# RG-LRU gate products as three passes over split operands, in a two-layer recurrent decoder step

## The chip, the cores and the metric

The kernel runs on one core of a Trainium2 chip. The metric is the device time of one execution in microseconds. Five engines work side by side, each through its own instructions in the order in which the program gives them: PE (TensorE, matmuls), DVE (VectorE), ACT (ScalarE), POOL (GpSimd) and SP (SyncE, which here only issues DMAs). An instruction waits until the semaphores that it names have been raised by other engines or by DMAs, and everything behind it on its engine waits with it.

## What is computed

Two layers run on 320 tokens (a prompt of 256 and eight samples of 8). Each layer normalizes its input, multiplies it with one wide matrix, feeds three branches (S5, RG-LRU, retention) and merges them. The change lies in the RG-LRU branch, whose reference is, shortened:

```python
xc = sum(xp[:, k:k + s] * cw[k] for k in range(CONV_WIDTH)) + conv_b
xb = xc.reshape(bsz, s, LRU_BLOCKS, LRU_BLOCK)            # 8 blocks of 128 channels
r = sigmoid(einsum('bsnc,ncd->bsnd', xb, w_a) + b_a)
i = sigmoid(einsum('bsnc,ncd->bsnd', xb, w_x) + b_x)
log_a = -LRU_C * r * softplus(-lam)
a = exp(log_a)
bx = sqrt(-expm1(2.0 * log_a)) * (i * xc)
h = scan(a, bx)
```

The two einsums are the gate products: per layer and per block of 128 channels one 128x128 matrix for `r` and one for `i`.

## The kernel before, in words

Everything is kept transposed: channels on the 128 partitions, tokens along the row. The program is one stream of weight blocks of 256 output channels (`blocks`, `stream`). A block is cut into chunks of four 128-row slices, a chunk into two half-chunks. A half-chunk is loaded in `raw` (SP issues the DMA, 512 KB for a whole chunk) and split by `split` into a high part (`whi`, ACT rounds it to float32r) and a low part (`wlo`, DVE subtracts); its matmuls are three passes, high by high, high by low of the input, low by high, at lines 1426 to 1428: 12 matmuls of 320 columns per half-chunk. Splits are prepared a few half-chunks ahead of PE (`lead`, 3 to 8), into four buffers and, in the first part of layer 0, five more that are called `more`.

Work beside the stream is written as Python generators that `step` advances after each half-chunk while the program is built; a `yield` gives the turn back, and `yield 0` goes on at once unless a running estimate of the load of DVE or ACT says that they are behind. So the place of an instruction on each engine is settled when the program is built. Nothing is reordered afterwards.

`lru_u` is such a generator. It runs once for each of the four pairs of LRU blocks (j = 0 to 3) in each layer, and in its order it

- writes the scaled input into `lu`, asks SP for the gate weights `lw` (two gates, two blocks, 128x128 each), 
- convolves on DVE, for each of the two blocks n, into `lxc` (128x344),
- runs four gate matmuls at line 805, two for n = 0 and, a chunk later, two for n = 1, float32 by float32 with 344 columns, into PSUM `ps`,
- takes the sigmoids on ACT into `lr` and `li`, and goes on to the scan and to the branch output `yhl`.

Tiles made by `wt` share a pool of ten buffers. Which of the ten a new tile gets is settled at build time, and its first writer then waits for the last reader of the tile that had the buffer, be it an engine or a DMA. Other users of the pool around the first gates (layer 0, j = 0) are the S5 input `u` and its two parts `uhi` and `ulo`, which `s5_u` stores to DRAM by three DMAs (`du`, `duh`, `dul`, line 497), and `s5b`, two loads of `s5_setup` (line 369). All of these DMAs stand in SP's queue, between the loads of `raw`.

Of the kernel before, what the change touches and what calls it, by code (L numbers as in the profile page):

```python
# [11 lines left out]
F32 = mybir.dt.float32  # L12
F32R = mybir.dt.float32r
# [18 lines left out]
CONVW = PADW - 3  # L32
# [46 lines left out]
class Program:  # L79
# [687 lines left out]
    def lru_u(self, l, j, pt):  # L767
        nc, I = self.nc, self.I
        u = self.wt([128, 2, PADW], name="lu")
        self.mul(u[:, :, 3:S0], pt[:, :, :SEQ], self.rs2()[:, :, :SEQ])  # L770
        us = u[:, :, S0:].rearrange("p n (b e) -> p n b e", e=11)
        for n in range(2):
            self.mul(us[:, n, :, 3:], pt[:, n, SEQ:T].rearrange("p (b s) -> p b s", s=NS),
                     self.rstd[:, SEQ:].rearrange("p (b s) -> p b s", s=NS))
        nc.vector.memset(u[:, :, 0:3], 0.0)
        while not self.flag.get(('lru', l)):
            yield
        for n in range(2):
            self.copy(us[:, n, :, 0:3], self.lin[:, 2 * j + n, 0:24].rearrange("p (b k) -> p b k", k=3))
        yield  # L780
        wg = self.wt([128, 2, 2, 128], name="lw")
        nc.sync.dma_start(wg, I['lw'][l, j])
        xc, r, i = [], [], []
        while j and not self.flag.get(('y', l, 0, j - 1)):
            yield
        for n in range(2):
            b = 2 * j + n
            x = self.vt([128, CONVW], name="lxc")
            self.ts(x, u[:, n, 0:CONVW], self.pcol(l, 'convw', b), OP.mult, self.pcol(l, 'convb', b), OP.add)
            for k in range(1, 4):  # L790
                yield 0
                self.stt(x, u[:, n, k:k + CONVW], self.pcol(l, 'convw', 8 * k + b), x, OP.mult, OP.add)
            xc.append(x)
            self.copy(self.lst[:, b, 9:12], u[:, n, SEQ:SEQ + 3])
            self.copy(self.lst[:, b, 12:36].rearrange("p (b k) -> p b k", k=3), us[:, n, :, 8:11])
            yield
        yield
        for n in range(2):
            b = 2 * j + n
            r.append(self.vt([128, CONVW + 8], name="lr"))  # L800
            i.append(self.vt([128, CONVW], name="li"))
            pp = []
            for k, dst, key in ((0, r[n][:, :CONVW], 'ba'), (1, i[n], 'bx')):
                p = self.ps()
                nc.tensor.matmul(p[:, :CONVW], wg[:, k, n], xc[n], start=True, stop=True)  # L805
                pp.append((dst, p, key))
            yield
            for dst, p, key in pp:
                self.act(dst, p[:, :CONVW], AF.Sigmoid, bias=self.pcol(l, key, b))
        yield  # L810
        while not self.flag.get(('sp', l)):
            yield
        for n in range(2):
            self.mul(i[n], i[n], xc[n])
            yield 0
        for n in range(2):
            self.act(xc[n], r[n][:, :CONVW], AF.Exp, scale=self.sp8[:, 2 * j + n:2 * j + n + 1])
        yield
        for n in range(2):
            t = r[n][:, :CONVW]  # L820
            self.act(t, t, AF.Tanh, scale=self.sp4[:, 2 * j + n:2 * j + n + 1])
        yield
        for n in range(2):
            self.stt(xc[n], xc[n], 1.0, r[n][:, :CONVW], OP.add, OP.mult)
            yield n
        for n in range(2):
            t = r[n][:, :CONVW]
            self.act(t, t, AF.Sqrt)
            self.ts(xc[n], xc[n], -1.0, OP.mult, 1.0, OP.add)
        yield  # L830
        for n in range(2):
            t = r[n][:, :CONVW]
            self.stt(t, xc[n], 1.0, t, OP.add, OP.mult)
            yield 0
            self.mul(i[n], i[n], t)
            nc.vector.memset(xc[n][:, S0 - 1:S0 + 77:11], 0.0)
            nc.vector.tensor_copy(i[n][:, S0 - 1:S0 + 77:11], self.lin[:, 2 * j + n, 24:32])
            yield 0
            self.dve(xc[n], 2.1)
            nc.vector.tensor_tensor_scan(r[n][:, :CONVW], xc[n], i[n], 0.0, op0=OP.mult, op1=OP.add)  # L840
            yield 0
        while not self.flag.get(('zl', l, j)):
            yield
        z = self.szl.pop(j)
        for n in range(2):
            h = r[n]
            self.copy(self.lst[:, 2 * j + n, 0:1], h[:, SEQ - 1:SEQ])
            self.copy(self.lst[:, 2 * j + n, 1:9], h[:, S0 + 7:S0 + 85:11])
            self.mul(z[:, n, :SEQ], z[:, n, :SEQ], h[:, :SEQ])
            zs = z[:, n, SEQ:].rearrange("p (b s) -> p b s", s=NS)  # L850
            self.mul(zs, zs, h[:, S0:S0 + 88].rearrange("p (b e) -> p b e", e=11)[:, :, 0:NS])
            yield 0
        self.y_parts(l, 0, j, z)
        self.nl += 1
        if self.nl == 4:
            yield
            nc.sync.dma_start(self.O['lru'][l], self.lst)
# [690 lines left out]
```

## Time and profile before

| | |
|---|---|
| median of 3 runs | 2372.26 us (2371.87 to 2372.94) |
| profiled execution, its own time | 2372.87 us |
| its span, first to last instruction | 2371.1 us |
| PE busy | 2349.4 us, 99% of the span |
| DVE busy | 1537.7 us, 65% |
| ACT busy | 1107.6 us, 47% |
| POOL busy | 606.3 us, 26% |
| chain that ended last | PE 98% |

The time of an execution is about 1.8 us longer than the span of its instructions. The profiled execution is 0.6 us slower than the median. PE has work in nearly every microsecond, and matmuls follow one another so closely that the recorded durations overlap; what one costs is read from start to start.

### The profile page before, as it was taken

How to read it: one execution, taken by the hardware profiler on the slowest of the kernel's cores; microseconds unless marked ns; L12 is line 12 of the kernel's file. 1: busy time of each engine (PE TensorE's matmuls, PEld its weight loads, DVE VectorE, ACT ScalarE, POOL GpSimd, SP SyncE). 2: the span in 40 equal slices, each digit the busy share in tenths (PEclk: the TensorE clock that was granted, in tenths of full speed). 3: DMA queues.
4: the chain of work that ended last, by engine and by line, in shares of the span. 5: the costliest groups of instructions: out<-in, count | busy, mean ns of one | idle time of the engine just before them, and what ended most of it. 6: DMA issues, size and time to landing. Idle time of an engine off the chain costs nothing.

```text
span 2371.1 us, 44404 instructions
## 1 busy us (share of the span) xinstructions
PE 2349.4 (99%) x16778; PEld 2324.5 (98%) x16778; DVE 1537.7 (65%) x2830; ACT 1107.6 (47%) x2021; POOL 606.3 (26%) x1159
## 2 busy tenths in 40 slices
PE   9999999999999999999999999999999999999997
PEld 8999999999999999999999999999999999999997
DVE  7886658677675657655557765856676656555544
ACT  6655644444443444344555564444444334444443
POOL 2020008999430000300100000699950300000011
PEclk9999999999999999999999999999999999999999
DMA  6745775465545545455656587454555554444453
GB/s 234 218 150 163 208 224 167 139 196 182 177 164 188 167 149 169 149 165 184 199 163 186 164 223 212 146 169 153 173 179 193 180 174 162 150 152 144 158 178 127
DMA packets 154023, 413.72 MB, mean 174 GB/s; under 512 B 18640, under 2 KB 60112, under 8 KB 153552
## 3 DMA queue, kind: packets, MB, share of 16 engines
q1 hardware_dynamic: 153232, 410.16, 54.5%
q8 instruction: 132, 2.16, 0.4%
q10 hardware_dynamic: 576, 0.72, 0.1%
q14 instruction: 83, 0.68, 0.1%
HBM read 373.83 MB, written 31.74 MB: 171 GB/s over the span
## 4 chain that ended last, share of the span: by engine, by line
PE 98%; DVE 1%; DMA 1%; ACT 0%; issue 0%; SPq 0%; ACTq 0%; DVEq 0%
PE pt L1426 31%; PE pt L1427 30%; PE pt L1428 30%; PE ps L678 1%; PE ps L805 1%; PE ps L581 1%; PE ps L1039 0%; PE ps L1111 0%; PE ps L1095 0%; PE ps L951 0%; PE ps L972 0%; DMA raw<-wb_lru 0%; PE ps L1078 0%; DMA xin<-x 0%; PE ps L670 0%
## 5 line engine op out<-in xcount | busy, mean ns | idle before, releaser
L98 DVE TENSOR_TENSOR wlo<-raw,whi 128x512 fp32r<-128x512 f32 (+1 forms) x1199 | 859.5, 726 | 746.0 <-ACT whi L125 729.5
L125 ACT ACTIVATE whi<-raw 128x512 fp32r<-128x512 f32 (+1 forms) x1199 | 745.6, 629 | 1019.8 <-PE pt L1427 864.9
L1426 PE MATMUL pt<-xh,whi 128*128 128x320 f32 x3352 | 1049.3, 313 | 1.2 <-ACT whi L125 1.1
L1427 PE MATMUL pt<-xl,whi 128*128 128x320 f32 x3352 | 1036.3, 309 | 1.2 <-DVE xl L118 1.2
L1428 PE MATMUL pt<-xh,wlo 128*128 128x320 f32 x3352 | 1036.3, 309 | 0.2 <-DVE wlo L98 0.2
L1426 PEld LDWEIGHTS pt<-xh,whi 128*128 128x128 f32 x3352 | 629.6, 188 | 7.2 <-issue 3.5
L1427 PEld LDWEIGHTS pt<-xl,whi 128*128 128x128 f32 x3352 | 629.7, 188 | 5.3 <-DVE xl L118 2.3
L1428 PEld LDWEIGHTS pt<-xh,wlo 128*128 128x128 f32 x3352 | 629.3, 188 | 0.9 <-DVE wlo L98 0.6
L1428 PE MATMUL pt<-yhl,wlo 128*128 128x320 f32 x768 | 238.0, 310 | 2.9 <-DVE wlo L98 2.9
L1426 PE MATMUL pt<-yhl,whi 128*128 128x320 f32 x768 | 238.9, 311 | 0.7 <-ACT yhl L125 0.7
L1427 PE MATMUL pt<-yhl,whi 128*128 128x320 f32 x768 | 238.1, 310 | 0.4 <-DVE yhl L98 0.4
L598 POOL TENSOR_TENSOR cs<-H,l2r 128x64 f32<-128x64 f32 x254 | 133.0, 524 | 240.4 <-DVE H L112 220.7
L271 POOL TENSOR_TENSOR acc<-acc,sq 128x320 f32<-128x320 f32 x28 | 25.6, 914 | 590.6 <-ACT sq L125 589.6
L1426 PE MATMUL pt<-M,whi 128*128 128x320 f32 x512 | 158.4, 309 | 0.0
L1428 PE MATMUL pt<-M,wlo 128*128 128x320 f32 x512 | 158.2, 309 | 0.0
L1427 PE MATMUL pt<-M,whi 128*128 128x320 f32 x512 | 158.2, 309 | 0.0
L1428 PEld LDWEIGHTS pt<-yhl,wlo 128*128 128x128 f32 x768 | 144.8, 189 | 3.2 <-DVE wlo L98 3.2
L1426 PEld LDWEIGHTS pt<-yhl,whi 128*128 128x128 f32 x768 | 144.8, 189 | 1.1 <-ACT yhl L125 1.0
L1427 PEld LDWEIGHTS pt<-yhl,whi 128*128 128x128 f32 x768 | 144.9, 189 | 0.7 <-DVE yhl L98 0.7
L599 POOL TENSOR_TENSOR cs<-H,l2i 128x64 f32<-128x64 f32 x254 | 127.8, 503 | 0.0
L601 POOL TENSOR_TENSOR H<-cs,cs 128x64 f32<-128x64 f32 x254 | 114.7, 452 | 19.9
L600 POOL TENSOR_TENSOR cs<-cs,H 128x64 f32<-128x64 f32 x254 | 119.5, 471 | 0.0
(255 smaller groups left out, 2445.1 us busy)
## 6 DMA issues: line engine op xcount, KB each, us to landing
raw<-w_in SPq DMA_DIRECT2D x447, 512.0 KB, 4.3
raw<-w_out SPq DMA_DIRECT2D x64, 512.0 KB, 4.3
raw<-wb_lru SPq DMA_DIRECT2D x32, 512.0 KB, 4.3
raw<-wb_ret SPq DMA_DIRECT2D x32, 512.0 KB, 3.7
raw<-wb_s SPq DMA_DIRECT2D x32, 512.0 KB, 3.6
r<-sret SPq DMA_DIRECT2D x16, 512.0 KB, 7.8
ret_s<-r SPq DMA_DIRECT2D x16, 512.0 KB, 3.0
raw<-w_glu SPq DMA_DIRECT2D x16, 512.0 KB, 3.6
```

What stands on the lines that cost most here:

```text
L98: self.nc.vector.tensor_tensor(o, a, b, op=op)
L125: self.nc.scalar.activation(o, a, f, **k)
L271: self.nc.gpsimd.tensor_tensor(self.acc, self.acc, sq, op=OP.add)
L581: self.nc.tensor.matmul(pp[g][:, a * HN:(a + 1) * HN], wst[:, a, g * 128:(g + 1) * 128], ust[:, 2 * a + g], start=True, stop=True, skip_gr ...
L598: g.tensor_tensor(t1, old, lr, op=OP.mult)
L599: g.tensor_tensor(t2, self.swap(old), li, op=OP.mult)
L600: g.tensor_tensor(t1, t1, new, op=OP.add)
L601: g.tensor_tensor(new, t1, t2, op=OP.add)
L678: nc.tensor.matmul(o[q * 32:(q + 1) * 32], w[:, c, m], H[:, q0 + m, c, col:col + HN], start=col == 1 and c == 0, stop=c == 1, tile_positio ...
L1426: nc.tensor.matmul(o, hi[:, kk, cs], xh, start=k == 0, stop=False)
L1427: nc.tensor.matmul(o, hi[:, kk, cs], xl, start=False, stop=False)
L1428: nc.tensor.matmul(o, lo[:, kk, cs], xh, start=False, stop=k == nk - 1)
```

## The change

`lru_u` no longer multiplies in float32. The gate weights are split once per j into `lwh` and `lwl`, and each `lxc` into the two halves of a tile `lxs`, by the same `split` as the main products (ACT copies, DVE subtracts). The four float32 matmuls of a pair become twelve in float32r with 344 columns each. The splits stand where one turn was given back before, and a `yield 0` follows each split of `lxc`.

```diff
         wg = self.wt([128, 2, 2, 128], name="lw")
         nc.sync.dma_start(wg, I['lw'][l, j])
+        wh = self.wt([128, 2, 2, 128], F32R, name="lwh")
+        wl = self.wt([128, 2, 2, 128], F32R, name="lwl")
         xc, r, i = [], [], []
...
-        yield
+        self.copy(wh, wg)
+        self.sub(wl, wg, wh.bitcast(F32))
+        yield
+        xs = []
+        for n in range(2):
+            xs.append(self.wt([128, 2, CONVW], F32R, name="lxs"))
+            self.split(xs[n][:, 0], xs[n][:, 1], xc[n])
+            yield 0
         for n in range(2):
...
                 p = self.ps()
-                nc.tensor.matmul(p[:, :CONVW], wg[:, k, n], xc[n], start=True, stop=True)
+                for a, w, c in ((0, wh, 0), (0, wh, 1), (1, wl, 0)):
+                    nc.tensor.matmul(p[:, :CONVW], w[:, k, n], xs[n][:, c], start=c == a == 0, stop=a == 1)
```

All four new tiles come from the pool of ten. In the built program of layer 0, j = 0, `lwh` and `lwl` get the two buffers that the two `s5b` tiles had before. The second `s5b` gets the buffer of `lu`, whose last reader is the convolution of n = 1. `lxs` of n = 0 gets the buffer of the S5 input `u`, last read by the DMA `du`; `lxs` of n = 1 gets that of `uhi`, last read by `duh`.

SP's queue, layer 0, from the third load behind `lw` to the stores of S5's j = 0, with the semaphores that each row waits for (DMAHW and a number is a DMA's, DVE, Pool and Activation an engine's). Before:

```order
L365 DMA s5t<-s5l 128x96
L369 DMA s5b<-s5b 128x512 [waits DMAHW2_49]
L369 DMA s5b<-s5b 128x512
L1330 DMA raw<-w_in 128x1024 [waits DMAHW4_49,DVE_49]
L497 DMA du<-u_772 128x2x338 [waits DMAHW5_49,Pool_49]
L497 DMA duh<-uhi 128x2x338 [waits DMAHW6_49]
```

Now:

```order
L365 DMA s5t<-s5l 128x96
L369 DMA s5b<-s5b 128x512 [waits DMAHW2_49,DVE_49,Pool_49]
L369 DMA s5b<-s5b 128x512 [waits DVE_49,Activation_49]
L1340 DMA raw<-w_in 128x1024 [waits DMAHW4_49]
L497 DMA du<-u_772 128x2x338 [waits DMAHW5_49,Pool_49]
L497 DMA duh<-uhi 128x2x338 [waits DMAHW6_49]
```

The order is the same; the second `s5b` load now waits for DVE (the convolution of n = 1), and the stores stand behind it.

ACT at the first gates (layer 0, j = 0); `more` and `whi` are high parts of main weights, `zs` a sigmoid for the S5 gate, `lr` the first sigmoid of the LRU gates:

```order
 L125 ACTIVATE lst<-lu 128x24
-L125 ACTIVATE more<-raw 128x512 x5
-L125 ACTIVATE zs<-z 128x640
+L125 ACTIVATE more<-raw 128x512 x3
+L125 ACTIVATE lwh<-lw 128x512
+L125 ACTIVATE more<-raw 128x512 x2
+L125 ACTIVATE zs<-z 128x640
+L125 ACTIVATE lxs<-lxc 128x344 x2
 L125 ACTIVATE whi<-raw 128x512 x2
 L125 ACTIVATE lr<-ps,pv_114 128x344
```

The two copies into `lxs` stand behind `zs`. On PE the gates keep their place there, behind the same 12 matmuls; the first needs the copy, the second the low part that DVE makes from it.

DVE around the gates of layer 0, j = 2, from the convolution of n = 1 on (`more` and `wlo` are low parts of main weights):

```order
 L114 TENSOR_SCALAR lxc<-lu,pv_114 128x344
 L118 SCALAR_TENSOR_TENSOR lxc<-lu,pv_114,lxc 128x344 x3
-L98 TENSOR_TENSOR wlo<-raw,whi 128x512
-L98 TENSOR_TENSOR more<-raw,more 128x512 x5
-L98 TENSOR_TENSOR wlo<-raw,whi 128x512 x2
...
+L98 TENSOR_TENSOR more<-raw,more 128x512 x2
+L98 TENSOR_TENSOR lwl<-lw,lwh 128x512
+L98 TENSOR_TENSOR more<-raw,more 128x512 x2
+L98 TENSOR_TENSOR lxs<-lxc,lxs 128x344 x2
+L98 TENSOR_TENSOR more<-raw,more 128x512
```

One `wlo` that stood behind the convolution now stands ahead of it, and the low parts of `lxs` stand behind four main splits and `lwl`. On PE the gates of j = 1 and 2 of layer 0 and of j = 1, 2 and 3 of layer 1 come 12 matmuls later than before; those of j = 0 and 3 of layer 0 and of j = 0 of layer 1 keep their place.

## Rows read from the trace of the kernel before

**Rows 1.** The page, busy time by engine and the chain that ended last:
```profile
PE 2349.4 (99%) x16778; PEld 2324.5 (98%) x16778; DVE 1537.7 (65%) x2830; ACT 1107.6 (47%) x2021; POOL 606.3 (26%) x1159
...
PE 98%; DVE 1%; DMA 1%; ACT 0%; issue 0%; SPq 0%; ACTq 0%; DVEq 0%
```

**Rows 2.** PE's waits, total us, times, longest:
```profile
PE pt L1428 <- DVE wlo L98: 3.1, 2, 2.9
```

**Rows 3.** PE by time around the first gates: start us, us, engine, line:
```profile
73.50 0.31 PE L1428 MATMUL pt<-xh,wlo 128*128 128x320 f32 x1
73.65 1.32 PE L805 MATMUL ps<-lxc,lw 128*128 128x344 f32 x4
74.55 0.57 PE L1426 MATMUL pt<-xh,more 128*128 128x320 f32 x1
74.96 0.30 PE L1427 MATMUL pt<-xl,more 128*128 128x320 f32 x1
```

**Rows 4.** All gate matmuls, records (two for each float32 matmul), ns min/median/max:
```profile
L805 PE MATMUL ps<-lxc,lw x64: 450/452/453, 73.7 to 1369.9; 128*128 128x344 f32 x64
```

**Rows 5.** SP by time, DMA issues around the first gates:
```profile
67.31 0.90 SPq L369 DMA_DIRECT2D s5b<-s5b  x2
69.80 0.33 SPq L1330 DMA_DIRECT2D raw<-w_in  x1
70.23 0.38 SPq L497 DMA_DIRECT2D du<-u  x1
70.66 0.46 SPq L497 DMA_DIRECT2D duh<-uhi  x1
```

**Rows 6.** DMAs: these two issues with us to landing, then all eight `du`:
```profile
du<-u SPq DMA_DIRECT2D x1, 338.0 KB, 7.2
...
duh<-uhi SPq DMA_DIRECT2D x1, 338.0 KB, 8.5
...
DMA to landing us min/median/max: 3.2/5.4/9.1
```

**Rows 7.** ACT by time, an activation of 128x344:
```profile
75.62 0.53 ACT L125 ACTIVATE lr<-ps,pv 128x344 f32<-128x344 f32 x1
```

**Rows 8.** DVE by time around the first gates:
```profile
69.69 1.19 DVE L118 SCALAR_TENSOR_TENSOR lxc<-lu,pv,lxc 128x344 f32<-128x344 f32 x2
...
72.00 0.51 DVE L98 TENSOR_TENSOR ulo<-u,uhi 128x338 fp32r<-128x338 f32 x1
```

**Rows 9.** DVE at j = 1 of layer 0, two multiplications while POOL works:
```profile
145.77 2.62 DVE L98 TENSOR_TENSOR li<-li,lxc 128x344 f32<-128x344 f32 x2
```

**Rows 10.** DVE, then PE, at the gates of layer 0, j = 2:
```profile
179.04 1.80 DVE L118 SCALAR_TENSOR_TENSOR lxc<-lu,pv,lxc 128x344 f32<-128x344 f32 x3
181.36 2.49 DVE L98 TENSOR_TENSOR more<-raw,more 128x512 fp32r<-128x512 f32 x4
...
180.35 1.32 PE L805 MATMUL ps<-lxc,lw 128*128 128x344 f32 x4
```

**Rows 11.** DVE, then PE, at the gates of layer 0, j = 3:
```profile
227.54 1.28 DVE L98 TENSOR_TENSOR wlo<-raw,whi 128x512 fp32r<-128x512 f32 x2
...
228.68 1.32 PE L805 MATMUL ps<-lxc,lw 128*128 128x344 f32 x4
```

**Rows 12.** DVE, then PE, at the gates of layer 1, j = 0:
```profile
1223.21 0.82 DVE L98 TENSOR_TENSOR z<-pt,rstd 128x640 f32<-128x640 f32 x1
...
1223.65 1.32 PE L805 MATMUL ps<-lxc,lw 128*128 128x344 f32 x4
```

**Rows 13.** PE around its longest wait, then four microseconds: us, busy by engine, PEclk, DMA:
```profile
955.81 0.41 PE L1428 MATMUL pt<-yhl,wlo 128*128 128x320 f32 x1 [2.91 <-DVE wlo L98]
...
957.21 0.47 PE L1426 MATMUL pt<-yhl,whi 128*128 128x320 f32 x1
957.48 0.47 PE L1427 MATMUL pt<-yhl,whi 128*128 128x320 f32 x1
...
956.00:960.00 4.00, 4.00 (x18) 4.00 (x18) 3.67 (x3) 0.30 (x1) 3.92 (x4) 0.57 0.31 85
```

## The prediction

> **What bounds the kernel now.** I read the busy times first, then the chain, then PE's waits, then the engines by time around the gates. PE is busy 99% of the span and the chain that ended last is PE for 98% [rows 1]. Its waits on other engines are small; the longest series, on low parts of weights, is 3.1 us in two waits [rows 2]. So a microsecond of PE work taken away is a microsecond saved, and one that PE waits is one lost: nothing later in the program is idle enough to give it back. DVE and ACT have room on average (65% and 47%), but in program order a short operation of theirs can still come late. The question is therefore what a gate pair costs PE now and then, and whether the new splits are ready when PE arrives.
>
> **What is removed.** From the start of the matmul ahead of the first gates (73.50) to the start of the second one behind them (74.96) pass 1.46 us, in which two main matmuls of 0.15 from start to start (73.50 to 73.65) also start [rows 3]: a pair costs PE 1.16 us. 64 records, two for each float32 matmul, are 32 matmuls or 16 pairs [rows 4], 18.6 us in all.
>
> **What PE gets instead.** Six float32r matmuls per pair, of 344 columns instead of 320. Nothing of that size in float32r is in the trace; scaled from 0.15 by 344/320 one is 0.16, a pair 0.97. The weights change with each one, as in the main stream. Saved: 0.19 per pair, 3.1 us in all. If the exact spacing is a hundredth of a microsecond more or less per matmul, it is 2.1 to 4.1. I take 3.1.
>
> The Trainium skill (FP8 and Floating Point Precision, TensorE Precision Notes) says that true float32 goes through the array in four passes. Three passes would then save a quarter of 1.16, or 4.6 us as an estimate, and the sum below would be 1.5 lower; the row gives the smaller value.
>
> **What ACT and DVE get.** Per j one weight split and two of `lxc`: 0.62 + 2 x 0.51 us on DVE [rows 8, 10] and about as much on ACT with 0.53 for 128x344 [rows 7]. That is some 13 us on each over the run, beside PE, and free but where PE stands waiting. Gates of n = 1 come two half-chunks behind those of n = 0, 24 matmuls or 3.6 us, so their splits are covered. For n = 0 I went through the eight places.
>
> **Layer 0, j = 0: the dear one.** The copy into the first `lxs` waits for the store `du`, which still reads that buffer. Before, `du` was issued at 70.23 [rows 5] and landed 7.2 us later [rows 6], at 77.4, when the gates (73.65) were long done. Now it is issued later: the second `s5b` load ahead of it needs the buffer of `lu`, which the convolution reads until 69.69 + 1.19 = 70.88 [rows 8]; before, it had gone by 68.2 [rows 5]. Behind it SP issues `s5b` (0.45), `raw` (0.43 to the next start) and then `du`, at 71.8. With 7.2 us it lands at 79.0. Then comes ACT's copy, 0.53 [rows 7], and DVE's low part, 0.51 [rows 8]: 80.0. PE's first pass would start at 73.65, the second, which needs the low part, at 73.81. PE waits 6.2 us. If the landing is set by the bytes queued ahead and stays at 77.4, it waits 4.6; with the longest of the eight `du` (9.1) it waits 8.1; with the shortest (3.2) 2.2. I take 6.2, since the row is of this very transfer.
>
> What else is queued there: behind the second copy, which waits for `duh` (72.2 + 8.5 = 80.7 [rows 6]), ACT has the next two `whi`, and SP has `raw` loads behind the stores. Five half-chunks are prepared at this place (`lead`), 60 matmuls or 9 us behind the gates, that is until 89; `whi` and `wlo` follow within 3 us of 80.7. I cost this at nothing; without that cover it would be up to those 3 us.
>
> **The other seven places.**
> Layer 0, j = 1: the low part comes out about when PE arrives, but POOL begins its S5 products here. Two DVE operations of 128x344 beside POOL took 2.62 us together [rows 9], 1.31 each instead of 0.51. One such loss is 0.8; I take 0.4, between 0 and 0.8.
> Layer 0, j = 2: before, the convolution ended at 179.04 + 1.80, one `wlo` followed, and four main splits began at 181.36 [rows 10]. That `wlo` now stands ahead of the convolution, so the splits still begin near 181.36. Four of them and `lwl`, 2.49 / 4 = 0.62 each, and then the low part: 181.36 + 3.1 + 0.51 = 185.0. PE's gates, 12 matmuls (1.8) later than 180.35, want it at 180.35 + 1.8 + 0.16 = 182.3. Wait 2.7. It is 0 if DVE, held by POOL before this place, gets further ahead of a later PE; but its splits can't run ahead of the buffers that PE frees, so I take 2.7.
> Layer 0, j = 3: `lwl` and two main splits from 227.54 on [rows 11], 3 x 0.62, then 0.51: 229.9, wanted at 228.84. Wait 1.1, between 0.5 and 1.3.
> Layer 1, j = 0: `z` on DVE ends at 1224.0 [rows 12], the low part at 1224.5, wanted at 1223.81. Wait 0.7, between 0.4 and 0.9.
> Layer 1, j = 1 to 3: the gates come 12 matmuls later and the splits, by the same counting, end before them: 0.
>
> **The clock.** When PE had idled 2.91 us, the granted clock fell soon after it resumed: over 956 to 960 it is 0.57 [rows 13], so some 3.4 us at the lower level (1.2 GHz), with matmuls 0.27 apart (957.21 to 957.48) instead of 0.15. That costs 3.4 x (1 - 0.15/0.27) = 1.5 us. The wait of 6.2 us is longer, so I add 1.5 once; 0 to 3.0 in all, as neither or both of the long waits pay.
>
> [...]
>
> **The sum.** -3.1 + 6.2 + 0.4 + 2.7 + 1.1 + 0.7 + 1.5 = +9.5 us. On the profiled execution's own 2372.87 that is 2382.4; it is 0.6 slower than the median, so I predict 2381.8.
>
> **Rivals.**
> "Early landing" ends on the other side. `du` lands after 3.2 us as the quickest one did; PE waits 2.2 and the clock holds: -3.1 + 2.2 + 0.4 + 2.7 + 1.1 + 0.7 = +4.0, 2376.3, no measurable change. It decides below a landing at about 75.7. For it speaks the spread of the eight, against it the 7.2 and 8.5 of just these transfers. 0.12.
> "Hidden": the splits and the store are ready everywhere and the change does only what PE's rows say, 2369.2. Against it is the store that lands behind the gates even in the old trace. 0.05.
> "No wait at j = 2": 2381.8 - 2.7 = 2379.1. 0.13.
> "Clock twice", or `du` later by as much: 2383.3 to 2385. 0.20.
> My forecast: 0.50.
>
> **Range and chances.** Down to 2374.5 it leaves out "hidden" and the better part of "early landing"; up to 2387 it takes in the longest `du` (+1.9) with the clock twice (+1.5) and the weaker saving (+1.0). A measurement of this kernel can tell about 0.2%, 4.7 us, from no change: slower begins at 2377.0, faster below 2367.5. Slower 0.83: the forecast, the two rivals above it or near it. Same 0.15: "early landing" and most of "hidden". Faster 0.02: "hidden" with the larger saving of 4.1 and a clean run.
>
> **What would show each step.** In the profile after: gate pairs of six matmuls 0.16 apart; a wait of PE at some 74 us of about 6 us, released by the low part of `lxs` on DVE, with ACT idle ahead of the copy until `du` lands; `du` issued near 71.8; waits of about 2.7, 1.1 and 0.7 at the gates of layer 0, j = 2 and 3, and layer 1, j = 0; none in the rest of layer 1; a lower granted clock for some 3 us behind the long wait. I am wrong if `du` lands early, if the float32r gates cost PE more than 1.16 a pair, or if PE waits later for weights that were held up behind ACT's wait.

## The result: 15 us slower, and where the rows put it

The changed kernel takes 2387.6 us at the median (2386.77 to 2388.8 in 4 runs) against 2372.28 us before: 1.0064 times as long, 95% interval 1.0052 to 1.0075. The forecast was +9.5 us with an upper end of 2387.0; the sign and the first mechanism were right, the size was not.

The page of the profile after, busy times:

```profile
PE 2353.8 (99%) x16810; PEld 2333.0 (98%) x16810; DVE 1549.9 (65%) x2854; ACT 1118.6 (47%) x2045; POOL 606.6 (25%) x1159
```

Little is seen in it: the busy shares are those of [rows 1] but for a point of POOL's, because PE at a lower clock counts as busy (4.00 of 4 us at 0.59 in the last row of the clock below) and 13 us of waiting in 2387 round away. The waits of PE tell more (us in total, times, longest):

```profile
PE ps L815 <- ACT lxs L125: 6.6, 2, 5.5
PE ps L815 <- DVE lxs L98: 6.5, 5, 2.8
PE pt L1438 <- DVE wlo L98: 1.9, 1, 1.9
```

The first two are new; the third answers to [rows 2]. All gate matmuls after, beside [rows 4]:

```profile
L815 PE MATMUL ps<-lxs,lwh x64: 314/320/655, 79.3 to 1387.0; 128*128 128x344 f32 x64
L815 PE MATMUL ps<-lxs,lwl x32: 313/320/488, 80.3 to 1387.2; 128*128 128x344 f32 x32
```

PE by time at a pair that waits for nothing (layer 0, j = 0, n = 1):

```profile
85.66 0.31 PE L1438 MATMUL pt<-xh,more 128*128 128x320 f32 x1
85.80 0.48 PE L815 MATMUL ps<-lxs,lwh 128*128 128x344 f32 x2
86.12 0.32 PE L815 MATMUL ps<-lxs,lwl 128*128 128x344 f32 x1
86.28 0.48 PE L815 MATMUL ps<-lxs,lwh 128*128 128x344 f32 x2
86.59 0.32 PE L815 MATMUL ps<-lxs,lwl 128*128 128x344 f32 x1
86.75 0.31 PE L1436 MATMUL pt<-xh,more 128*128 128x320 f32 x1
```

Six passes take from 85.80 to 86.75, 0.95 us, where a pair took 1.16. The saving is there. Now the first gates, SP, ACT, DVE and PE by time, to be read beside [rows 3, 5, 7, 8]:

```profile
67.37 3.91 SPq L369 DMA_DIRECT2D s5b<-s5b  x2
...
71.85 0.38 SPq L497 DMA_DIRECT2D du<-u  x1
...
78.80 0.49 ACT L125 ACTIVATE lxs<-lxc 128x344 fp32r<-128x344 f32 x1 [3.60 <-DMA du<-u]
...
79.33 0.52 DVE L98 TENSOR_TENSOR lxs<-lxc,lxs 128x344 fp32r<-128x344 f32 x1 [3.69 <-ACT lxs L125]
...
73.52 0.31 PE L1438 MATMUL pt<-xh,wlo 128*128 128x320 f32 x1
79.35 1.21 PE L815 MATMUL ps<-lxs,lwh 128*128 128x344 f32 x2 [5.51 <-ACT lxs L125]
...
81.50 0.47 PE L1436 MATMUL pt<-xh,more 128*128 128x320 f32 x1
81.76 0.47 PE L1437 MATMUL pt<-xl,more 128*128 128x320 f32 x1
```

SP stands at `s5b` for 3.9 us, `du` goes out at 71.85 and lands at 78.8, ACT copies, PE starts its first pass on the copy and its second, 0.55 later, on the low part, and its main matmuls run 0.27 apart instead of 0.15. The place that the forecast left too cheap is layer 0, j = 2: DVE, then PE, beside [rows 10].

```profile
188.39 1.80 DVE L118 SCALAR_TENSOR_TENSOR lxc<-lu,pv,lxc 128x344 f32<-128x344 f32 x3
190.12 1.29 DVE L98 TENSOR_TENSOR more<-raw,more 128x512 fp32r<-128x512 f32 x2
191.32 0.68 DVE L98 TENSOR_TENSOR lwl<-lw,lwh 128x512 fp32r<-128x512 f32 x1
191.92 1.29 DVE L98 TENSOR_TENSOR more<-raw,more 128x512 fp32r<-128x512 f32 x2
193.12 0.94 DVE L98 TENSOR_TENSOR lxs<-lxc,lxs 128x344 fp32r<-128x344 f32 x2
...
189.12 0.31 PE L1438 MATMUL pt<-xh,more 128*128 128x320 f32 x1
190.51 0.43 PE L815 MATMUL ps<-lxs,lwh 128*128 128x344 f32 x1 [1.08 <-ACT lxs L125]
193.69 0.65 PE L815 MATMUL ps<-lxs,lwh 128*128 128x344 f32 x1 [2.75 <-DVE lxs L98]
```

PE waits twice in one pair, and stretches of the clock (us, busy by engine, PEclk, DMA) show the same drop as [rows 13] behind it:

```profile
184.00:190.00 6.00, 5.43 (x38) 5.16 (x36) 5.34 (x13) 3.59 (x11) 0.00 (x0) 1.00 0.65 206
190.00:196.00 6.00, 2.74 (x9) 2.50 (x10) 4.67 (x9) 1.36 (x4) 0.00 (x0) 0.71 0.48 152
196.00:200.00 4.00, 4.00 (x19) 4.00 (x18) 0.69 (x1) 1.49 (x3) 0.00 (x0) 0.59 0.47 166
```

To place the whole difference I took the start of the same main matmul in both traces and subtracted. The forecast beside it is its wait and clock less 0.39, the saving of two pairs.

| stretch | forecast, us | measured, us |
|---|---|---|
| layer 0, j = 0 | 7.3 | 7.25 |
| layer 0, j = 1 | 0.0 | -0.1 |
| layer 0, j = 2 | 2.3 | 6.45 |
| layer 0, j = 3 | 0.7 | 1.5 |
| rest of layer 0 (most of it at 955 us) | 0 | -1.25 |
| layer 1, j = 0 | 0.3 | 0.35 |
| layer 1, j = 1, 2, 3 | -0.4 each | -0.3, 0.7, 0.75 |
| rest of layer 1 | 0 | 0.6 |
| sum (spans 2371.1 and 2387.0) | 9.4 | 15.9 |

### The profile page after: what moved, and what is told of

It reads as the page before. It is cut to its first block, busy times and chain, and to the rows that moved or that the text cites. A ratio compares the mean times of both kernels' runs of the same rounds, so it can differ in the third digit from the quotient of the medians.

```text
span 2387.0 us, 44526 instructions
## 1 busy us (share of the span) xinstructions
PE 2353.8 (99%) x16810; PEld 2333.0 (98%) x16810; DVE 1549.9 (65%) x2854; ACT 1118.6 (47%) x2045; POOL 606.6 (25%) x1159
## 4 chain that ended last, share of the span: by engine, by line
PE 88%; DVE 1%; issue 0%; ACT 0%; DVEq 0%; ACTq 0%
PE pt L1436 28%; PE pt L1437 27%; PE pt L1438 27%; PE ps L678 1%; PE ps L581 1%; DVE wlo L98 0%; PE ps L815 0%; PE ps L1049 0%; PE ps L1121 0%; PE ps L1105 0%; PE ps L961 0%; PE ps L982 0%; PE ps L1088 0%; PE ps L670 0%; DVE yt L98 0%
```

## Experiments

The first theory of the excess at j = 2: PE's 7 us stall at j = 0 upsets DVE's work for S5, and j = 2 is its echo. Evidence was one reversal on POOL. POOL multiplies S5's input matrix in nine products beside the LRU work of j = 1 (`cmul` in `s5_setup`, lines 454 to 458), and also clears the padding of S5's `u` (line 487). Before, the third product (the first row of line 458) stood ahead of the third clearing; now it stands behind it. POOL before, then after:

```profile
134.90 1.32 POOL L458 TENSOR_TENSOR bb<-bb,s5bt 128x512 f32<-128x512 f32 x1
145.57 0.17 POOL L487 MEMSET u<- 128x36 f32 x1 [9.36 <-issue]
...
156.86 1.45 POOL L458 TENSOR_TENSOR bb<-bb,s5bt 128x512 f32<-128x512 f32 x1
```

```profile
152.73 0.17 POOL L487 MEMSET u<- 128x36 f32 x1 [7.88 <-DVE u L98]
152.81 1.31 POOL L458 TENSOR_TENSOR bb<-bb,s5bt 128x512 f32<-128x512 f32 x1
...
165.54 1.47 POOL L458 TENSOR_TENSOR bb<-bb,s5bt 128x512 f32<-128x512 f32 x1
```

The last product ends 8.7 us later than before, PE at that point is 7.15 us later: 1.55 us too late. DVE's operations take longer beside POOL ([rows 9]), so DVE comes late too.

**Own room for the split tiles of layer 0, j = 0 to 2.** They move behind the five `more` pairs, in the same tile.

```diff
-self.more = self.ph.tile([128, 5, 2, 2, 256], F32R, name="more", tag="H")
+self.room = self.ph.tile([128, 9920], F32R, name="more", tag="H")
+self.more = self.room[:, :5120].rearrange("p (u s k c) -> p u s k c", u=5, s=2, k=2)
...
+if l == 0 and j < 3:
+    o = 5120 + 2400 * (j % 2)     # wh, wl and both lxs from self.room at o
```

> The split weights and split inputs of layer 0, j = 0 to 2, get room of their own (behind the five extra weight pairs in the tile that these use), so the first copy waits for no store. Theory: the 6.9 us at the first gates are all the wait for the store of u, and the late splits at j = 2 are its echo (DVE's S5 columns came late, POOL's third product fell behind the clearing of u, DVE beside it lost 1.6 us). Then no wait over 0.3 us at j = 0, under 3.5 us instead of 5.1 at j = 2, and 2376.5 to 2378.5 us. Rival: the splits at j = 2 are late by their own work on DVE, whatever came before; then j = 2 keeps its 5.1 us and the time is 2379.5 to 2381. Second rival: the first splits come late in any case (DVE has them behind other work); then 1 us or more of the wait at j = 0 stays.

Measured 2383.04 us (ratio 1.0043, 1.0027 to 1.0060), 4.6 less than the changed kernel. At j = 0 ACT, DVE and PE (the split tiles are parts of `more` here):

```profile
74.34 0.74 ACT L125 ACTIVATE zs<-z 128x640 f32<-128x640 f32 x1 [2.80 <-DVE z L98]
74.98 0.85 ACT L125 ACTIVATE more<-lxc 128x344 fp32r<-128x344 f32 x2
...
75.97 0.93 DVE L98 TENSOR_TENSOR more<-lxc,more 128x344 fp32r<-128x344 f32 x2
...
75.51 0.42 PE L822 MATMUL ps<-more 128*128 128x344 f32 x1 [1.26 <-ACT more L125]
76.53 1.05 PE L822 MATMUL ps<-more 128*128 128x344 f32 x5 [0.60 <-DVE more L98]
```

The store was the larger part; behind it stood a second wait of some 2.4 us, since the copy queues behind `zs`, which waits for DVE's `z`. And j = 2 costs 6.35 us, by the starts of the same matmuls, as good as the 6.45 of the changed kernel. The echo theory is refuted: without the stall POOL's third product still stands behind the clearing (147.93), because the order was settled when the program was built. The time lies above every range expected, since both costs stayed in part or whole.

**Splits alone.** All splits run, the gates are the float32 matmuls of before.

```diff
-for a, w, c in ((0, wh, 0), (0, wh, 1), (1, wl, 0)):
-    nc.tensor.matmul(p[:, :CONVW], w[:, k, n], xs[n][:, c], start=c == a == 0, stop=a == 1)
+nc.tensor.matmul(p[:, :CONVW], wg[:, k, n], xc[n], start=True, stop=True)
```

> All splits and tiles of the change stay, but the gates are the float32 matmuls of before, on the unsplit weights and inputs, so PE reads no split part. Theory: what costs time is only PE standing at the gates for a split part; ACT standing for the store is hidden by the weights prepared ahead. Then 2371.5 to 2373.5 us, no new wait of PE. Rival: ACT's stall or DVE's extra work makes later weights late; then PE waits on high or low parts of weights after 80 us, and the time is 2375 us or more.

2371.85 us, ratio 0.9998 (0.9989 to 1.0007). The added work, 9.5 us on ACT and 11.1 on DVE by their busy times, costs nothing where PE reads no split part. The other half of the theory was not put to the test, because ACT did not stand for the store in this kernel. Its first copy runs right behind `zs` and waits for no DMA, while `du` goes out as late as in the changed kernel (71.59):

```profile
74.86 0.47 ACT L125 ACTIVATE lxs<-lxc 128x344 fp32r<-128x344 f32 x1
```

What ACT's stall costs behind the gates has to be read from the changed kernel itself, below.

**The clearing of u on DVE**, everything else as in the change.

```diff
-nc.gpsimd.memset(u[:, :, :, HP:HC:5], 0.0)
+nc.vector.memset(u[:, :, :, HP:HC:5], 0.0)
```

> The changed kernel with one difference: the small clearing of S5's u runs on DVE instead of POOL, so that POOL's products don't stand behind it. Theory: at j = 1 POOL's third product then runs near 146 us instead of 152.8, POOL's row of products ends earlier, DVE is free earlier and the gates of layer 0, j = 2 cost 3.5 us or less instead of 5.1; the time is 2385.5 to 2386.5 us, the 6.9 us at j = 0 stay. Rival: DVE is late at j = 2 by its own added splits; then the wait there and the time (2387.6) don't move by over 0.5 us.

2382.95 us (1.0043, 1.0028 to 1.0058), 4.65 less, more than twice the forecast: j = 2 costs 0.75 us for 6.45, j = 0 0.95 more. POOL, then PE at j = 2:

```profile
145.53 1.32 POOL L458 TENSOR_TENSOR bb<-bb,s5bt 128x512 f32<-128x512 f32 x1
...
158.24 1.47 POOL L458 TENSOR_TENSOR bb<-bb,s5bt 128x512 f32<-128x512 f32 x1
...
189.88 0.32 PE L815 MATMUL ps<-lxs,lwh 128*128 128x344 f32 x1
191.09 0.42 PE L815 MATMUL ps<-lxs,lwh 128*128 128x344 f32 x1 [0.90 <-DVE lxs L98]
```

POOL no longer stands for DVE's `u` at all and is done 7.3 us sooner, so this is more than an undoing. j = 2 waits 1.05 us, and its drop of the clock is gone with the long wait.

**Gates two half-chunks later** (`yield` ahead of the gate loop).

> The changed kernel with the gates two half-chunks of the main stream (24 matmuls, 3.5 us) further behind their splits, everywhere. Theory: the landing of the store and the end of the splits are fixed, so every wait shrinks by 3.5 us: at j = 0 PE arrives at 77.2 and waits about 2.2 us for the copy and 0.4 for the low part, at j = 2 about 1.6, nowhere else; 2372 to 2375 us. Rival: the later gates push their readers on ACT and DVE, and new waits for weights or for the branch's outputs eat it; then 2376 us or more, with waits at other lines.

2410.79 us (1.0160, 1.0145 to 1.0176). At the gates the theory held in the main: 1.9 + 0.4 us at j = 0 and nothing at six of the eight places, j = 2 among them, where 1.6 had been expected. At layer 0, j = 3, PE waits 4.0 us for DVE's work on S5 weights, and behind that stands a store once more: DVE had waited for ACT's copy of n = 1, and ACT for `dw`, a store of S5 weights.

```profile
249.16 0.49 ACT L125 ACTIVATE lxs<-lxc 128x344 fp32r<-128x344 f32 x1 [5.01 <-DMA dw<-w]
```

But PE's waits now begin with

```profile
PE pt L1437 <- ACT yhl L125: 21.9, 2, 12.1
```

j + 1 begins its convolution only when the branch output of j is made, so the delays add up over j, and the last output of each layer comes some 10 us after PE wants it. The rival was right, far beyond its price.

**Own room and the clearing on DVE.**

> Own room for the split tiles of layer 0, j = 0 to 2, and the clearing of u on DVE, with the splits where the change has them. Theory: the two causes are independent, each mend takes what it took alone (4.6 us each from 2387.6): 2376 to 2378.5 us, with 2.4 us of wait left at j = 0, 1.2 at j = 2 and 1.9 at j = 3. Rival: they share a part (a stall at j = 0 is what makes j = 2 late); then 2379 us or more.

2378.4 us (1.0026, 1.0016 to 1.0037). 2387.6 - 4.6 - 4.65 is 2378.35: the two causes are independent. In the profiled executions j = 0 costs 3.5 us here and 1.95 with own room alone, although PE waits 2.4 both times: here the clock fell behind these waits (0.57 granted from 77 to 81 us), there it did not (1.00).

**The kernel before with the clearing on DVE.**

> The kernel before with the clearing of u on DVE and nothing else. Theory: PE waits nowhere for what the clearing holds up there, so the time does not change: 2371.5 to 2373 us. Rival: the clearing on POOL costs the kernel before something too, so that the mend is worth its 4.6 us, or a part over 1 us, without the change: 2371 us or less.

2371.84 us (0.9997, 0.9988 to 1.0007). In the order of the kernel before the clearing on POOL costs nothing.

**Splits uncounted.** The planner's sums for DVE and ACT, the running estimate of load that `yield 0` looks at, are restored after each split, so that all other work stands where it stood.

```diff
+kept = dict(self.load)
 self.split(xs[n][:, 0], xs[n][:, 1], xc[n])
+self.load = kept
```

> The changed kernel with its splits left out of the planner's sums for DVE and ACT, so that every other piece of work and the gates stand where they stood before the change. Theory: POOL's third product stands ahead of the clearing again, which takes the 4 us at layer 0, j = 2 away, but the gates of five places come 12 matmuls (1.8 us) earlier and meet splits that are not ready: 2389 to 2393 us with waits of 2 to 3 us at layer 0, j = 1 and 2, and layer 1, j = 1 to 3. Rival: the counted load is what made the changed kernel slow; then 2384 us or less.

2392.88 us (1.0083, 1.0069 to 1.0097), inside the range expected. The third product stands ahead of the clearing again, and the last one ends as late as PE is at that point (11.5 us). The gates of five places come 1.8 us sooner to their splits. Already at j = 1, where the changed kernel waited some 0.3 us, PE now waits

```profile
142.93 0.65 PE L819 MATMUL ps<-lxs,lwh 128*128 128x344 f32 x1 [2.36 <-DVE lxs L98]
```

At j = 2 the pair takes 3.9 us longer than one that waits for nothing. Less the 1.8 that is 2.2 at the place of the changed kernel, near the 2.7 forecast; there PE waits 4.3, by its starts (from where a matmul would have followed to where it did). So the order that the counted splits brought about is what made j = 2 dear. This run put back the order on DVE and PE together with POOL's and doesn't single one out; that it goes by POOL and the clearing rests on the clearing on DVE, and on the pair of runs near the end that differ in the clearing alone. The time itself came out by other parts than expected: j = 0 cost 0.8 more than in the changed kernel, and in layer 1 PE waits 1.9, 0.9 and 1.1 us at j = 1 to 3, where 2 to 3 had been expected.

**All mends, splits earlier.** Own room in both layers, the clearing on DVE, and the splits inside the convolution loop. (S5's state `H`, which takes that room over, now starts only behind the gates of j = 3.)

```diff
 for n in range(2):
...
+    if n == 0:
+        self.copy(wh, wg)
+        self.sub(wl, wg, wh.bitcast(F32))
+    xs.append(own[n])
+    self.split(xs[n][:, 0], xs[n][:, 1], xc[n])
     yield
-self.copy(wh, wg)
-self.sub(wl, wg, wh.bitcast(F32))
 yield
```

> All three mends at once: split tiles in room of their own in both layers, the clearing of u on DVE, and the splits for n = 0 (its weights' too) right behind the convolution of n = 0, ahead of that of n = 1. Theory: no gate waits any more, and what is left is PE's saving, 16 pairs x 0.22 = 3.5 us, and up to 1 us at 955 us, where every changed kernel so far waited less than the kernel before: 2367.5 to 2369.5 us, faster than both. Rival: the earlier splits hold up the second convolution or ACT's weight copies, and new waits of 2 us or more come at the gates of n = 1 or at the main stream; then 2371 us or more.

2393.51 us (1.0093, 1.0079 to 1.0107). No gate waits, each pair takes 0.95. But the gates went back, 36 matmuls at j = 0 and 94 at j = 3 of layer 0. I put that down to the load of the splits, now counted inside the convolution loop; no run shows it by itself. And

```profile
PE pt L1442 <- ACT yhl L125: 14.8, 2, 9.6
```

is the wait of the later gates again. With the clearing left on POOL:

> As the kernel with all three mends, but the clearing of u stays on POOL. Theory: POOL's third product still falls behind it and DVE comes 1.6 us late to layer 0, j = 2, but the earlier splits give more than 3 us there, so this costs nothing: 2367.5 to 2370 us. Rival: at j = 2 the convolution of n = 0 itself ends behind PE's arrival; then a wait of 1 to 3 us stays at this one place, and the time is 2369.5 to 2372.

2392.31 us (1.0088, 1.0074 to 1.0103); it has the same 14.8 us and decides nothing about the clearing.

**The same with the last `yield` dropped**, which brings the gates forward:

> Own room for the split tiles, the clearing of u on DVE, the splits for n = 0 behind the convolution of n = 0, and one pause fewer ahead of the gates, so that these come 12 matmuls later than in the kernel before at the first place and 24 to 58 earlier at the others of layer 0. Theory: the splits are in time and the branch's outputs come no later than before, so only PE's saving is left, 16 pairs x 0.22 = 3.5 us, with up to 1 us at 955 us: 2367.5 to 2369.5 us. Rival: gates this early meet their splits again, with 1 us or more at several of the eight places: 2371 to 2378 us.

2368.3 us (0.9984, 0.9975 to 0.9993): faster than both kernels, though against the kernel before by less than the 0.2% that the forecast took as measurable. The only wait left at a gate is for a sigmoid that frees PSUM:

```profile
PE ps L817 <- ACT lr L125: 1.1, 1, 1.1
```

**That with the clearing on POOL**, and **that with float32 gates** (diff as for splits alone):

> The same with the clearing of u left on POOL. Theory: the third product stands behind the clearing and DVE comes late to layer 0, j = 2, but now DVE's lateness is covered by the earlier splits: within 1 us of the kernel with the clearing on DVE. Rival: the lateness is not covered; then 1.5 to 5 us more at layer 0, j = 2 and nowhere else.

> The kernel with all mends and the sooner gates, but its gates are float32 matmuls on the unsplit tiles as before; the splits still run and nothing reads them. It prices the passes by themselves at a place where nothing waits. Theory: 3.5 us more than the same kernel with split gates, 16 pairs x 0.22, so 2371 to 2373 us. Rival: the gain of that kernel comes from its order and its room, not from the passes; then this one is within 1 us of it.

With the clearing on POOL 2372.04 us (0.9997, 0.9988 to 1.0006), 3.7 more, by one row at layer 0, j = 2, and what follows on it:

```profile
177.33 1.60 PE L817 MATMUL ps<-more 128*128 128x344 f32 x6 [2.41 <-ACT more L125]
```

The theory that the lead covers it was wrong, its rival right. With float32 gates 2371.55 us (0.9995, 0.9987 to 1.0004), 3.25 more: that is the price of the passes by themselves, 16 x 0.21 = 3.4 from the rows.

## Why the prediction missed

**PE's saving: right.** 3.1 forecast (2.1 to 4.1), 3.4 from the rows, 3.25 between two kernels that differ in the passes alone. The Trainium skill (FP8 and Floating Point Precision, TensorE Precision Notes) says four passes for float32, from which I estimated 4.6. The rows differ from that estimate: a float32r pass of 344 columns takes 0.158, not the quarter of 0.58 that a float32 matmul takes, so three of them save less. How much of the difference is the change of weights at each pass, no run shows.

**Layer 0, j = 0: right, by its steps.** `du` issued at 71.85 (71.8 forecast), landed at 78.8 (79.0), copy, low part, one drop of the clock; 7.25 us against 7.3. PE's first pass stood too, for the copy; the forecast let only the second one stand, which changes nothing in the sum. What stood behind the store, 2.4 us for `zs` and `z`, the forecast hadn't seen; "early landing" would have met it. And the bounds of this step were misread: the 3.2 and 9.1 of [rows 6] come from the eight loads that read `du` back into `yu` (line 665), which that row takes in with the stores. The kernel before, the stores of layer 0 by themselves, then these loads:

```profile
DMA to landing us min/median/max: 5.6/5.7/7.2
DMA to landing us min/median/max: 3.2/3.4/9.1
```

The stores of layer 1 landed after 5.3 to 6.4. So no store landed as early as "early landing" says, nor as late as the end of the range allows.

**Layer 0, j = 2: the step that failed.** "That `wlo` now stands ahead of the convolution, so the splits still begin near 181.36" took DVE to arrive with PE. With PE 7.15 later that is 188.5; they began at 190.12. The order on DVE had been read around this place alone. POOL's, 40 us earlier, had not, though it is known before any run: a product behind a clearing, because the splits count in the planner's sums. The first low part came at 193.6 for 192.15. Counted by starts PE stood from 189.27 to 190.51 and from 190.67 to 193.69, 4.3 us for 2.7. That one took the clock as well: the five passes from 193.69 last 1.6 us for 0.8, and the fifteen main matmuls behind them, 0.27 apart up to 199.3 us, lose another 1.8. So "clock twice" was right on the clock, 2.6 us for the second time. The Trainium skill (TensorE: Matmul & The Clock Gate, Why this matters for your kernels) warns against idle gaps of PE between bursts of matmuls, behind which it falls back to half its clock. The rows behind both long waits agree: 0.59 granted from 80 to 84 us, 0.71 and 0.59 from 190 to 200. Wait and clock at j = 2 together are 4.2 of the 6.4 us that the sum missed in the profiled execution.

**Layer 1, j = 2 and 3: 2.3 us missed.** I had counted 0. The step "the splits, by the same counting, end before them" failed too. In the new order the product `z` stands ahead of the low part, behind two splits of main weights (j = 2):

```profile
1332.36 1.29 DVE L98 TENSOR_TENSOR wlo<-raw,whi 128x512 fp32r<-128x512 f32 x2
1333.56 0.82 DVE L98 TENSOR_TENSOR z<-z,zs 128x640 f32<-128x640 f32 x1
1334.30 0.94 DVE L98 TENSOR_TENSOR lxs<-lxc,lxs 128x344 fp32r<-128x344 f32 x2
1334.87 0.43 PE L815 MATMUL ps<-lxs,lwh 128*128 128x344 f32 x1 [0.81 <-DVE lxs L98]
```

**Layer 0, j = 3: 0.8 missed.** DVE came 0.76 late: `lwl` began at 241.91, where the 227.54 of [rows 11] and PE's 13.61 would be 241.15. In the new order the low part of the branch output `yhl` (at 234.22, 0.82 us) stands ahead of the convolution of j = 3. **Layer 1, j = 0 and 1, and layer 0, j = 1: right** within 0.15. **ACT's stall costs nothing behind the gates: right**, by the rows of the changed kernel: from the gates of j = 0 to those of j = 1 (87 to 141 us) PE stays 7.27 to 7.28 us behind the kernel before. The splits alone say nothing on it.

**At 955 us** the wait of [rows 2] fell from 2.9 to 1.9 in the changed kernel, which gave back 1.1 us by the starts. The drop of the clock behind it stayed: 0.59 granted over the four microseconds from 970, for 0.57 in [rows 13]. Why its order shortens the wait was not pursued, nor the 0.6 us in the rest of layer 1.

## What to carry to other kernels

A new operation on an engine with spare time cost nothing here until a busy engine read its result; then price the whole queue ahead of it, buffers and stores included. Where the same program code also weighs load, a split that is free in time still moves other engines' instructions: compare the order on every engine, also far ahead of the place. Giving the consumer more time is not the cure when a chain runs from it to an output that is also wanted: start the producer earlier instead, and keep the consumer no later than it was.

## What the runs showed that was not expected

A 0.17 us clearing on POOL is worth 4.65 us or nothing, by what stands behind it: 2387.6 to 2382.95 in the changed kernel, 2372.28 to 2371.84, no measurable change, in the one before. And the price of a wait is not in proportion to its length: 4.3 us of waiting at j = 2 cost 2.6 more by the clock, while 1.05 us at the same place cost none. Nor does the length alone decide: 2.4 us of waiting at j = 0 took the clock in one kernel and not in another, and the 1.9 us at 955 us took it as well.
